# The second product of a squared-ReLU MLP by seven products of halves, with the context's part in a stage of its own

## The chip, the cores and the metric

The kernel runs on one core of one Trainium2 chip as one program. The metric is the device time of one execution in microseconds (us); lower is better. Time before: 4007.97 us, median of three runs (3997.19 to 4012.74).

## The reference, cut to what matters

Two layers of a block with a mixer and an MLP over 1024 tokens of width 1024, and 256 context tokens whose MLP runs in the first layer alone:

```python
def sq_relu_mlp(h, w1, w2):
    a = jax.nn.relu(h @ w1)          # w1: 1024 x 4096
    return (a * a) @ w2              # w2: 4096 x 1024

for l in range(DEPTH):               # DEPTH = 2
    ...
    hx = modulate(rmsnorm(xl, norm2_g[l]), m[:, 3], m[:, 4])
    xl = xl + m[:, 5] * sq_relu_mlp(hx, mlp_w1[l], mlp_w2[l])
    if not last:
        ...
        xc = xc + mc[5] * sq_relu_mlp(hc, mlp_w1[l], mlp_w2[l])
return rmsnorm(xl, final_g)
```

Everything is float32. The change is in the second product, `(a * a) @ w2`, and in what the first one hands to it.

## The kernel before

**Pieces.** The 1024 tokens are two pieces of 512, A and B; the context is a piece C of 256. Activations lie with features on the 128 partitions and tokens along the row, so one matmul has 128 x 128 weights and 512 (C: 256) moving columns.

**Three matmuls for one.** Each float32 operand is cut into a high part (ACT copies it to the matmul's format, L251) and a low part (the difference, on POOL for weights, L291, on DVE for the hidden values, L1771). `mm3` (L254) then issues hi x hi, hi x lo and lo x hi into one bank: called a *three* below.

**Up.** `up` (L1603) makes the hidden values in 16 steps n of two blocks of 128 features, already by seven products of halves of A and B (the weights' sums on DVE, their cuts on ACT and POOL, L1568 to L1582). The products are added on DVE (L1621), squared after the ReLU on DVE (L1625) or ACT, and four results of a step are stored to DRAM in `h` (one of two blocks for one piece each), with two for C.

**Down.** `mlp` (L1785) runs `down` (L1799) over groups of four blocks of w2's rows (at the end groups of two); for each group over the pieces A, C, B (layer 1: A, B) and the eight output blocks b, with one three for each block of the group. After a group's block DVE adds the bank, times a gate, to the residual (L1544, tiles xrA, xrB, xrC). `down_parts` (L1748) makes ready the next group while this one runs: the hidden values `hraw` are loaded, and cut into mhA, mhB or mhC; a row block of w2 (128 x 1024) is loaded in two pieces of 128 x 512 and cut into whi and wlo. In layer 0 `mod_part` (L459, L462) also runs through both stages: it loads `wmod` and adds it up on DVE and POOL for the next layer's gates.

**The end.** In layer 0 A and C are normed for layer 1 (L534, L545) within the last groups, and B after the last matmul, which layer 1's first product of B needs. In layer 1 the final norm, the transposes (L1863), the last scaling (L1865) and the output follow.

**What sets the order.** The code's order is that in which work is recorded; a scheduler fixes each engine's own order. All DMAs go through SP's queue in program order, over eight semaphore lanes; an issue that must wait for a buffer or a lane keeps everything behind it.

## Time and profile before

| | us |
|---|---|
| median of three runs | 4007.97 (3997.19 to 4012.74) |
| the profiled execution | 4004.61 |
| its span in the profile | 4002.8 |
| PE busy | 3587.2 (90%) |
| down of layer 0, with C | 1775.8 to 2224.6 |
| the next layer's first matmul of B | 2259.6 |
| down of layer 1 | 3631.6 to 3981.6 |

The span is the time from the program's first to its last instruction as the profiler saw it; the rest of the execution lies around it. Places in the span are given in us from its start. Stages follow one another on PE, so a stage is read by itself: its stretch of the span, who is busy all through it, and what PE waits for at its two ends.

### The profile page before, as it was taken

To read this page: it belongs to the slowest core of one execution; us is meant where nothing else is said; L and a number is where in the kernel's file an instruction comes from. 1 tells how busy PE (TensorE), PEld (TensorE's weight loads), DVE (VectorE), ACT (ScalarE), POOL (GpSimd) and SP (SyncE) were. 2 spreads that over 40 slices of the span, in tenths; PEclk is the share of its full clock that TensorE was granted. 3 is DMA by queue.
4 is the path that set the end of the run, shared out by engine and by line. 5 is a ranking of instruction groups with operands and counts; after the bars stand their busy time and mean duration, and the time that the engine had idled before them with its cause. 6 is when DMAs were issued, how large, how long until landed. Compare 5 with 4: busy or idle time off the path is not lost.

```text
span 4002.8 us, 61327 instructions
## 1 busy us (share of the span) xinstructions
PE 3587.2 (90%) x23646; PEld 3007.7 (75%) x23646; DVE 2574.5 (64%) x4120; ACT 1394.9 (35%) x2547; POOL 1381.4 (35%) x982
## 2 busy tenths in 40 slices
...
GB/s 220 113 122 138 124 112 176 144 134 113 138 158 203 89 125 142 135 230 150 91 106 35 82 143 88 120 103 180 111 144 149 157 170 95 116 136 188 87 95 42
DMA packets 511174, 520.56 MB, mean 130 GB/s; under 512 B 34454, under 2 KB 384162, under 8 KB 510882
## 3 DMA queue, kind: packets, MB, share of 16 engines
...
## 4 chain that ended last, share of the span: by engine, by line
PE 54%; DVE 11%; DMA 3%; issue 2%; POOL 2%; ACT 2%; SPq 0%; DVEq 0%; ACTq 0%; POOLq 0%
PE bank L254 53%; DVE iD L835 1%; DVE iE L836 1%; DVE iD L829 1%; DMA wmod<-in_w_mod_dram 1%; DMA wraw<-in_mlp_w_dram 0%; DMA yin<-y 0%; POOL macc L462 0%; PE bank L1195 0%; POOL wlo L291 0%; PE bank L258 0%; POOL ras L1153 0%; DVE nt L275 0%; DVE iF L837 0%; DVE rsv L1327 0%
## 5 line engine op out<-in xcount | busy, mean ns | idle before, releaser
L291 POOL TENSOR_TENSOR wlo<-wraw,whi 128x512 fp32r<-128x512 f32 x360 | 503.1, 1420 | 1251.4 <-ACT whi L251 554.6
L251 ACT ACTIVATE whi<-wraw 128x512 fp32r<-128x512 f32 x360 | 214.2, 623 | 369.1 <-PE bank L254 165.8
L254 PE MATMUL bank<-mhB,whi 128*128 128x512 f32 x1024 | 316.2, 390 | 0.0
L254 PE MATMUL bank<-mhA,whi 128*128 128x512 f32 x1024 | 315.4, 389 | 0.0
L1544 DVE SCALAR_TENSOR_TENSOR xrB<-bank,mod,xrB 128x512 f32<-128x512 f32 x176 | 131.6, 749 | 218.9 <-PE bank L254 218.8
L1568 POOL TENSOR_TENSOR uS<-us,uS 128x512 fp32r<-128x512 f32 x128 | 194.3, 1528 | 194.0 <-ACT uS L251 176.2
L254 PEld LDWEIGHTS bank<-mhA,whi 128*128 128x128 f32 x1024 | 192.1, 188 | 39.7
L254 PEld LDWEIGHTS bank<-mhB,whi 128*128 128x128 f32 x1024 | 191.5, 188 | 39.1
L1544 DVE SCALAR_TENSOR_TENSOR xrA<-bank,mod,xrA 128x512 f32<-128x512 f32 x176 | 130.3, 746 | 121.5 <-PE bank L254 121.3
L1621 DVE TENSOR_TENSOR ms<-bank,ms 128x512 f32<-128x512 f32 x216 | 145.1, 684 | 95.5 <-PE bank L254 88.8
L462 POOL TENSOR_TENSOR macc<-macc,wmod 128x512 f32<-128x512 f32 x84 | 135.8, 1616 | 200.9 <-ACT wmod L251 198.1
L459 DVE SCALAR_TENSOR_TENSOR macc<-wmod,cs,macc 128x512 f32<-128x512 f32 x140 | 141.1, 1008 | 98.4 <-DMA wmod<-in_w_mod_dram 54.1
L254 PE MATMUL bank<-xhA,whi 128*128 128x512 f32 (+1 forms) x480 | 203.6, 425 | 0.0
L254 PE MATMUL bank<-xlA,whi 128*128 128x512 f32 (+1 forms) x480 | 199.6, 417 | 0.3 <-POOL xlA L538 0.3
L254 PE MATMUL bank<-xhA,wlo 128*128 128x512 f32 (+1 forms) x480 | 199.0, 416 | 0.6 <-POOL wlo L291 0.6
L254 PE MATMUL bank<-mhB,wlo 128*128 128x512 f32 x512 | 199.3, 389 | 0.0
L254 PE MATMUL bank<-mhA,wlo 128*128 128x512 f32 x512 | 199.2, 389 | 0.0
L254 PE MATMUL bank<-xhB,whi 128*128 128x512 f32 (+1 forms) x416 | 165.5, 398 | 13.7 <-ACT ru L251 13.7
L702 DVE SCALAR_TENSOR_TENSOR gy<-gu,vt,gy 128x1282 f32<-128x1282 f32 (+1 forms) x96 | 154.3, 1607 | 27.1 <-ACT gy L251 26.4
L254 PE MATMUL bank<-xlB,whi 128*128 128x512 f32 (+1 forms) x416 | 164.5, 395 | 0.0
L254 PE MATMUL bank<-xhB,wlo 128*128 128x512 f32 (+1 forms) x416 | 164.3, 395 | 0.0
L1568 POOL TENSOR_TENSOR uA<-wraw,uA 128x512 fp32r<-128x512 f32 x96 | 140.4, 1472 | 60.3 <-ACT uA L251 57.5
...
## 6 DMA issues: line engine op xcount, KB each, us to landing
...
wraw<-in_w_in_dram SPq DMA_DIRECT2D x100, 256.0 KB
...
```

The source lines that it names most:

```text
L251: return self.S.activation(out, in_, func, **kw)
L254: return self.nc.tensor.matmul(out, lhsT, rhs, start=start, stop=stop)
L291: self.P.tensor_tensor(lo[:, o + i:o + i + m], raw, h.bitcast(F32), SUB)
L459: V.scalar_tensor_tensor(acc[:, 0], raw, c[0], acc[:, 0], MUL, ADD)
L462: P.tensor_tensor(acc[:, 1], acc[:, 1], raw, ADD)
L702: V.scalar_tensor_tensor(y[:, a:b], u[:, a + t:b + t], w(t), y[:, a:b], MUL, ADD)
L829: (V.tensor_copy if d else self.act)(lane(D, 3 * d, i, 4), lg[d][q[i], :, q[i]])
L835: V.tensor_tensor(t, F[:, m:, j:m].to_broadcast([128, n, m]), E[:, j:m, :m].to_broadcast([128, n, m]), MUL)
L836: V.tensor_tensor(E[:, m:, :m], E[:, m:, :m], t, SUB)
L1544: self.V.scalar_tensor_tensor(x, ps, self.lv[self.l]["m"][:, mo + b, i:i + 1], x, MUL, ADD)
L1568: self.P.tensor_tensor(t[:, 1], w, t[:, 0].bitcast(F32), SUB)
L1621: V.tensor_tensor(out, ps, s, ADD)
```

## The change

**Seven products for eight.** `halves_down` takes w2 in halves (of the hidden features even and odd blocks, of the output blocks 0 to 3 and 4 to 7) and the tokens in halves A and B, and forms the eight products of halves by seven. It runs 112 steps in each layer: two halves f of the hidden features, seven products p, eight pairs of blocks n. A step holds one sum of weights cut in two (`wu`, 128 x 512) and one part of the hidden values cut in two (`hu`, 128 x 512) and does four threes of 512 columns, one into each of four banks, which gather over the eight n. At n == 7 the banks are added into the running sums `ms` or into the residual (`out`). The weights lie whole as loaded (`we`, `wo`, 128 x 1024 each, eight of both); their sums are made on DVE at p == 1 (in the recorded order), one of them in tiles `ws`, and f = 1's weights are loaded into the same tiles at p == 3 and p == 6.

**Up stores seven parts.** Each step of `up` stores the four results and three differences of them (T1 to T4 with T4 in the next step), made on DVE; three of the four squares are on ACT now.

**The context first.** `context_down` does C's product before, in 32 iterations of eight threes of 256 columns, a column block of w2 at a time (wraw pieces of 128 x 4 x 128: rows of 512 bytes), with one of the two low parts on DVE. C is then normed for layer 1, and stored.

**The end.** The squares of B's blocks 4 to 7 are made before the last product's banks, those of 0 to 3 after it.

```diff
+HALVES = ("B11", "B21", "T2", "T3", "T4", "T1", "B22")
+DOWN = ("A11", "A12", "S2", "S3", "A22", "S1", "S4")
...
-                self.P.tensor_tensor(lo[:, o + i:o + i + m], raw, h.bitcast(F32), SUB)
+                (self.V if even and i else self.P).tensor_tensor(lo[:, o + i:o + i + m], raw, h.bitcast(F32), SUB)
...
-        if j:
+        if len(sq) > 1:
...
+        def keep(t, n, i):
+            self.store(self.dram(f"h{l}{n}", (128, 7, 512))[:, HALVES.index(i)], t)
...
+        def square(t):
             self.act(t, t, AF.Relu)
             self.act(t, t, AF.Square)
+            return t
...
+            if rest:
+                c21, t2 = rest.pop()
+                t = tile()
+                V.tensor_tensor(t, c21, t2, SUB)
+                keep(t, n - 1, "T4")
+                self.free(t, c21, t2)
             if ready:
+                c11 = tile()
+                self.load(c11, self.dram(f"h{l}{n}", (128, 7, 512))[:, 0])
                 if n % 2:
                     self.free(s1s[n // 2])
             else:
                 ps = prod("A12", "B21")
                 ctx(0, "A12", 1)
-                third(total(s1, ps, s1), n, 0, 0)
+                c11 = square(total(s1, ps, s1))
+                keep(c11, n, "B11")
...
             u4 = total(tile(), prod("S1", "T1"), u2)
             done("S1")
             ps = prod("S3", "T3")
-            t = total(tile(), ps, u4)
+            c22 = total(tile(), ps, u4)
             total(u2, ps, u2)
-            second(t, n, 1, 512)
+            keep(square(c22), n, "B22")
             done("S3")
-            second(total(u4, prod("S4", "B22"), u4), n, 0, 512)
+            c12 = total(u4, prod("S4", "B22"), u4)
+            V.scalar_tensor_tensor(c12, c12, 0.0, c12, ALU.max, MUL)
             done("S4")
             next(mod, None)
             ps = prod("A22", "T4")
...
                 ctx(1, "A22", 1)
                 ctx(1, "A21", 0)
                 self.free(x["A21"])
+            t1, t2 = tile(), tile()
+            V.tensor_tensor(t1, c12, c11, SUB)
+            keep(t1, n, "T1")
+            V.tensor_tensor(t2, c22, t1, SUB)
+            keep(t2, n, "T2")
+            V.tensor_tensor(c12, c22, c12, SUB)
+            keep(c12, n, "T3")
+            self.free(t1, c11, c22, c12)
             done("A22")
-            second(total(u2, ps, u2), n, 1, 0)
+            c21 = square(total(u2, ps, u2))
+            keep(c21, n, "B21")
+            rest.append((c21, t2))
...
+    def context_down(self, l, mod):
+        V = self.V
         w2 = self.A["mlp_w2"][l].rearrange("(k p) c -> p k c", p=128)
+        hs, ws = [], {}
+        for n in range(16):
+            while not (self.avail["x"] or self.avail["w"]) or n >= 12 and self.upward:
+                yield
+            t = self.slot("mhC", (2, 2, 256), F32R, "a")
+            raw = self.slot("hraw", (2, 256), F32, "r")
+            self.load(raw, self.dram(f"hc{l}{n}", (128, 2, 256)))
             self.act(t[:, 0], raw)
+            V.tensor_tensor(t[:, 1], raw, t[:, 0].bitcast(F32), SUB)
             self.free(raw)
+            hs.append(t)
+            if n % 4 == 3 and n < 12:
+                while len(self.avail["u"]) < 2:
+                    yield
+                ws[n // 4] = self.wsplit(w2[:, n // 4 * 8:n // 4 * 8 + 8, 0:128], kind="u")
+                yield
+        self.back_x(f"xm{l}", "C")
+        for i in range(32):
+            b, c = divmod(i, 4)
+            if i + 3 < 32:
+                d, e = divmod(i + 3, 4)
+                ws[i + 3] = self.wsplit(w2[:, e * 8:e * 8 + 8, d * 128:d * 128 + 128], kind="u", even=True)
+            if c == 0:
+                ps = self.ps("d")[:, :256]
+            hi, lo = ws.pop(i)
+            for k in range(8):
+                t = hs[c * 4 + k // 2]
+                self.mm3(ps, hi[:, k], lo[:, k], t[:, 0, k % 2], t[:, 1, k % 2], c == 0 and k == 0, c == 3 and k == 7)
+            self.free(hi, lo)
+            if b == 7:
+                self.free(*hs[c * 4:c * 4 + 4])
+            if c == 3:
+                self.residual(b, 40)(ps, "C")
+            if i % 2:
+                next(mod, None)
             yield
+    def halves_down(self, l, last):
+        V = self.V
+        w2 = self.A["mlp_w2"][l].rearrange("(k p) c -> p k c", p=128)
+        take = lambda nm, kind, dt=F32: self.slot(nm, (2, 512), dt, kind)
+        steps = [(f, p, n) for f in range(2) for p in range(7) for n in range(8)]
+        raws, us, hs = {}, [], []
+        even, odd, sums = [], [], []
+        def fetch(t, fb):
+            self.load(t, w2[:, fb].rearrange("p (h c) -> p h c", h=2))
+        def fetch_h(i):
+            if i < len(steps):
+                f, p, n = steps[i]
+                raws[i] = self.slot("hraw", (512,), F32, "r")
+                self.load(raws[i], self.dram(f"h{l}{8 * f + n}", (128, 7, 512))[:, p])
+        def ready(i):
+            if i >= len(steps):
+                return
+            f, p, n = steps[i]
+            fetch_h(i + 5)
+            w = {"A11": (even, 0), "A12": (odd, 0), "S2": (even, 0), "S3": (even, 1), "A22": (odd, 1), "S4": (odd, 0)}
+            src = sums[n // 2][:, n % 2] if DOWN[p] == "S1" else w[DOWN[p]][0][n][:, w[DOWN[p]][1]]
+            u, h, raw = us[i % 3], hs[i % 3], raws.pop(i)
+            self.act(h[:, 0], raw)
+            V.tensor_tensor(h[:, 1], raw, h[:, 0].bitcast(F32), SUB)
+            self.free(raw)
+            self.act(u[:, 0], src)
+            self.P.tensor_tensor(u[:, 1], src, u[:, 0].bitcast(F32), SUB)
+            if p == 1:
+                e, o, s1 = even[n], odd[n], sums[n // 2][:, n % 2]
+                V.tensor_tensor(s1, e[:, 1], o[:, 1], ADD)
+                V.tensor_tensor(e[:, 1], e[:, 0], e[:, 1], SUB)
+                V.tensor_tensor(e[:, 0], s1, e[:, 0], SUB)
+                V.tensor_tensor(o[:, 0], o[:, 0], e[:, 0], SUB)
+            for q, ts, o in ((3, even, 0), (6, odd, 1)):
+                if p == q:
+                    if f == 0:
+                        fetch(ts[n], 2 * (n + 8) + o)
+                    else:
+                        self.free(ts[n])
+            if p == 5 and f == 1 and n % 2:
+                self.free(sums[n // 2])
+        def wait(kind, n=1):
+            while len(self.avail[kind]) < n:
+                yield
+        for i in range(8):
+            yield from wait("x")
+            even.append(take("we", "x"))
+            fetch(even[i], 2 * i)
+            if i == 3:
+                for j in range(5):
+                    fetch_h(j)
+        yield
+        for i in range(8):
+            yield from wait("u")
+            odd.append(take("wo", "u"))
+            fetch(odd[i], 2 * i + 1)
+        while self.upward:
             yield
+        yield "turn"
+        for i in range(3):
+            us.append(take("wu", "x", F32R))
+            hs.append(take("hu", "xuu"[i], F32R))
+        ready(0)
+        ready(1)
+        u2, u3 = ([take("ms", "x") for _ in range(2)] for _ in range(2))
+        sums += [take("ws", "w!") for _ in range(4)]
+        half = lambda t, b: t[b // 2][:, b % 2]
+        def out(b, pc, ps, s):
+            t = self.slot("mt", (512,), kind="r")
+            V.tensor_tensor(t, ps, s, ADD)
+            x = self.block(self.xr[pc], b)
+            V.scalar_tensor_tensor(x, t, self.lv[self.l]["m"][:, 40 + b, 0:1], x, MUL, ADD)
+            self.free(t)
+        for i, (f, p, n) in enumerate(steps):
+            ready(i + 2)
+            if n == 0:
+                ps = [self.ps("d") for _ in range(4)]
+            u, h = us[i % 3], hs[i % 3]
+            for b in range(4):
+                c = slice(b * 128, b * 128 + 128)
+                self.mm3(ps[b], u[:, 0, c], u[:, 1, c], h[:, 0], h[:, 1], n == 0, n == 7)
+                if n == 7:
+                    a, z = half(u2, b), half(u3, b)
+                    nm = DOWN[p]
+                    if nm == "A11":
+                        self.act(a, ps[b])
+                    elif nm == "A12":
+                        out(b, "A", ps[b], a)
+                    elif nm == "S2":
+                        V.tensor_tensor(a, ps[b], a, ADD)
+                    elif nm == "S3":
+                        V.tensor_tensor(z, ps[b], a, ADD)
+                    elif nm == "A22":
+                        out(b + 4, "A", ps[b], z)
+                    elif nm == "S1":
+                        V.tensor_tensor(a, ps[b], a, ADD)
+                        out(b + 4, "B", ps[b], z)
+                    else:
+                        out(b, "B", ps[b], a)
+            if f == 1 and n == 7 and p == 5:
+                self.free(*u3)
+            yield f, p, n
+        self.free(*u2, *us, *hs)
     def mlp(self, l, last):
         mod = iter(()) if last else self.mod_part(l + 1, 0, 48)
+        down = self.halves_down(l, last)
+        self.upward = True
+        if last:
+            self.up(l, last, mod, down)
+        else:
+            ctx = self.context_down(l, mod)
+            self.up(l, last, mod, ctx)
+            turn = ""
+            for i, _ in enumerate(ctx):
+                if i > 8 and not turn:
+                    turn = next(down)
+            for _ in mod:
+                pass
+            self.gains(l + 1, 1)
+            self.rstat("C")
+            self.norm(l + 1, 1, "C")
+            self.save_x(f"x{l + 1}", "C")
+            del self.xr["C"]
+        while last and next(down) != "turn":
+            pass
+        for p in "AB":
             self.back_x(f"xm{l}", p)
+        sq = []
+        for f, p, n in down:
+            if f == 0:
+                continue
+            if (p, n) == (5, 1):
                 self.rstat("A")
+            if (p, n) == (5, 7) and not last:
+                self.first = [self.wsplit(self.win(l + 1, c), kind="w!") for c in (768, 256)]
+            if (p, n) == (6, 0):
+                if not last:
+                    self.norm(l + 1, 1, "A")
+                for j in (2, 3):
+                    self.squares("B", j, sq)
+        for j in range(2):
+            self.squares("B", j, sq)
+        self.rsum("B", sq)
         if not last:
             self.norm(l + 1, 1, "B")
```

**SP, layer 0, about the end of up.** Names are the tile written, then what is read: hraw are hidden values, wraw a weight piece, wmod the gates' weights, we and wo the whole row blocks of w2. Before:

```order
L261 DMA hraw<-h_10711 128x2x256
L261 DMA hraw<-h_10770 128x2x256
L261 DMA hraw<-h_10711 128x512 x2
L261 DMA hraw<-h_10770 128x512 x2
L261 DMA wmod<-in_w_mod_dram 128x512 x5
L261 DMA hraw<-h_11600 128x512
L261 DMA wraw<-in_mlp_w_dram 128x512 x2
L261 DMA hraw<-h_11600 128x512
L261 DMA wraw<-in_mlp_w_dram 128x512 x2
L261 DMA hraw<-h_11830 128x512
```

After, the loads that follow the last ones of the context's stage:

```order
L264 DMA wraw<-in_mlp_w_dram 128x4x128 x8
L264 DMA wmod<-in_w_mod_dram 128x512 x3
L264 DMA wraw<-in_mlp_w_dram 128x4x128 x4
L264 DMA wmod<-in_w_mod_dram 128x512 x3
L264 DMA wraw<-in_mlp_w_dram 128x4x128 x2
L264 DMA wmod<-in_w_mod_dram 128x512 x2
L264 DMA wo<-in_mlp_w_dram 128x1024 x2
L264 DMA we<-in_mlp_w_dram 128x1024 x2
L264 DMA wo<-in_mlp_w_dram 128x1024 x6
L267 DMA x_15725<-xrC_14422 128x4x256
L267 DMA x_15725<-xrC_14423 128x4x256
L264 DMA xrA_15728<-xm_10026 128x2x512
```

The weights of the halves' stage (wo and the last two we, 512 KB each) stand behind all loads of the context's stage, and the reload of the residual (xrA and on) behind them.

**DVE, layer 0, from the context's last bank to the second step of the halves.** In the rows of after L1849 is a sum of the last weights loaded, L277 to L279 the last rounds of the rsqrt, L537 and L548 the norm of C, L1842 the low part hu of a step. Before, a steady stretch of down:

```order
L1544 SCALAR_TENSOR_TENSOR xrB_14200<-bank_70,mod_116,xrB_14200 128x512
L1544 SCALAR_TENSOR_TENSOR xrB_14201<-bank_71,mod_116,xrB_14201 128x512
L1771 TENSOR_TENSOR mhA<-hraw,mhA 128x512
L1544 SCALAR_TENSOR_TENSOR xrB_14201<-bank_72,mod_116,xrB_14201 128x512
L471 TENSOR_TENSOR mod_117<-bank_74,vt_114 128x4
L1771 TENSOR_TENSOR mhA<-hraw,mhA 128x512 x2
L1544 SCALAR_TENSOR_TENSOR xrA_14186<-bank_67,mod_116,xrA_14186 128x512
```

After:

```order
L1849 TENSOR_TENSOR we<-we 128x512
L279 SCALAR_TENSOR_TENSOR rst_2_360<-nt_0_366,rst_2_360 128x2
L277 TENSOR_TENSOR nt_0_366<-rst_2_360 128x2
L278 TENSOR_TENSOR nt_0_366<-nt_0_366,nh_0_368 128x2
L279 SCALAR_TENSOR_TENSOR rst_2_360<-nt_0_366,rst_2_360 128x2
L537 SCALAR_TENSOR_TENSOR nt<-xrC_14422,g_1_131,bank_73 128x256 x3
L548 SCALAR_TENSOR_TENSOR xlC_15685<-nt,mod_117,xhC_15683 128x256
L537 SCALAR_TENSOR_TENSOR nt<-xrC_14422,g_1_131,bank_73 128x256
L548 SCALAR_TENSOR_TENSOR xlC_15685<-nt,mod_117,xhC_15683 128x256
L537 SCALAR_TENSOR_TENSOR nt<-xrC_14423,g_1_131,bank_73 128x256 x4
L548 SCALAR_TENSOR_TENSOR xlC_15686<-nt,mod_117,xhC_15684 128x256
L1842 TENSOR_TENSOR hu<-hraw,hu 128x512
```

The second step's hu now stands behind that sum and nearly the whole norm of C; before, an mhA has only residuals and the gates' sums about it.

**DVE, after, in layer 0 from the first half f = 0 to f = 1** (before's down has no such sums; its steady rows stand above):

```order
L1848 TENSOR_TENSOR ws<-we,wo 128x512 x2
L1842 TENSOR_TENSOR hu<-hraw,hu 128x512
L1849 TENSOR_TENSOR we<-we 128x512 x2
L1848 TENSOR_TENSOR ws<-we,wo 128x512 x2
L1842 TENSOR_TENSOR hu<-hraw,hu 128x512
L1849 TENSOR_TENSOR we<-we 128x512 x2
L1848 TENSOR_TENSOR ws<-we,wo 128x512
L1842 TENSOR_TENSOR hu<-hraw,hu 128x512
L1849 TENSOR_TENSOR we<-we 128x512
L1848 TENSOR_TENSOR ws<-we,wo 128x512 x2
L1849 TENSOR_TENSOR we<-we 128x512
L1842 TENSOR_TENSOR hu<-hraw,hu 128x512
```

Four steps' hu stand here with thirteen sums of f = 1's weights; with the rows up to the next hu it is five steps and sixteen sums.

## Rows read from the trace of the kernel before

**Rows 1.** Stretches of up's start, up, down (layer 0), down (layer 1), and their columns.

```profile
core 0: us, PE busy (x) PEld busy (x) DVE busy (x) ACT busy (x) POOL busy (x), PEclk, DMA share, GB/s
...
1350.00:1400.00 50.00, 39.29 (x183) 31.22 (x182) 46.39 (x58) 29.32 (x53) 27.60 (x17) 0.83 0.32 96
1500.00:1600.00 100.00, 100.00 (x543) 86.80 (x542) 62.24 (x77) 40.06 (x74) 61.67 (x42) 1.00 0.44 140
...
1876.00:1976.00 100.00, 100.00 (x536) 86.81 (x535) 54.54 (x73) 19.78 (x35) 24.59 (x16) 1.00 0.37 116
3736.00:3836.00 100.00, 100.00 (x443) 82.84 (x442) 43.15 (x57) 20.55 (x36) 22.92 (x16) 1.00 0.32 100
```

**Rows 2.** Line L254 over the span: count, durations, first and last start.

```profile
L254 PE MATMUL bank<-mhA,whi x1024: 387/389/486, 1775.8 to 3968.5; 128*128 128x512 f32 x171
```

**Rows 3.** Groups of layer 0's MLP (1335 to 2260): C's matmuls.

```profile
L254 PE MATMUL bank<-mhC,whi 128*128 128x256 f32 x512 | 92.8, 284 | 0.1
```

**Rows 4.** Timeline of PE: threes of 512 (layer 1's first) and of 256 columns.

```profile
2203.68 0.40 PE L254 MATMUL bank<-mhC,whi 128*128 128x256 f32 x2
...
2205.84 0.40 PE L254 MATMUL bank<-mhC,whi 128*128 128x256 f32 x2
...
3631.64 0.62 PE L254 MATMUL bank<-mhA,whi 128*128 128x512 f32 x2
...
3633.68 0.62 PE L254 MATMUL bank<-mhA,whi 128*128 128x512 f32 x2
```

**Rows 5.** The page's groups: busy, mean ns of one, idle before.

```profile
L291 POOL TENSOR_TENSOR wlo<-wraw,whi 128x512 fp32r<-128x512 f32 x360 | 503.1, 1420 | 1251.4 <-ACT whi L251 554.6
L251 ACT ACTIVATE whi<-wraw 128x512 fp32r<-128x512 f32 x360 | 214.2, 623 | 369.1 <-PE bank L254 165.8
...
L1544 DVE SCALAR_TENSOR_TENSOR xrA<-bank,mod,xrA 128x512 f32<-128x512 f32 x176 | 130.3, 746 | 121.5 <-PE bank L254 121.3
```

**Rows 6.** Timelines of DVE and of POOL in up, 1644 to 1647 us.

```profile
1644.32 1.76 DVE L1574 TENSOR_TENSOR us<-wraw 128x512 f32<-128x512 f32 x1 [1.19 <-POOL uS L1568]
...
1646.61 0.68 DVE L1575 TENSOR_TENSOR us<-us,wraw 128x512 f32<-128x512 f32 x1
...
1644.24 1.30 POOL L1568 TENSOR_TENSOR uA<-wraw,uA 128x512 fp32r<-128x512 f32 x1
```

**Rows 7.** Stretches with DMA at full load; columns as in rows 1.

```profile
1174.00:1182.00 8.00, 6.79 (x37) 5.36 (x35) 6.50 (x21) 4.75 (x8) 3.53 (x3) 1.00 1.11 298
...
1780.00:1800.00 20.00, 20.00 (x100) 16.97 (x99) 9.24 (x12) 8.67 (x14) 9.11 (x6) 1.00 1.01 347
1800.00:1820.00 20.00, 19.88 (x124) 17.86 (x124) 16.57 (x25) 5.32 (x9) 3.75 (x3) 1.00 0.80 267
```

**Rows 8.** Timeline of SP ahead of the first of these stretches: the loads issued.

```profile
1173.38 9.31 SPq L261 DMA_DIRECT2D wraw<-in_w_out_dram  x8
```

**Rows 9.** Timelines at layer 0's end: last down matmul, norms, B's first.

```profile
2224.25 0.39 PE L254 MATMUL bank<-mhB,wlo 128*128 128x512 f32 x1
...
2232.78 1.06 ACT L251 ACTIVATE sq<-xrB 128x1024 f32<-128x1024 f32 x1 [0.62 <-DVE xrB L1544]
...
2236.12 1.23 DVE L496 TENSOR_TENSOR sq<-sq 128x1024 f32<-128x1024 f32 x1
...
2237.40 2.31 PE L254 MATMUL bank<-cst,sq 128*128 128x1 f32 x16 [1.14 <-DVE sq L496]
...
2240.28 1.26 DVE L534 SCALAR_TENSOR_TENSOR nt<-xrC,g,bank 128x256 f32<-128x256 f32 x3 [0.16 <-PE bank L258]
...
2245.13 0.70 DVE L270 TENSOR_SCALAR rst<-rsm 128x4 int32<-128x4 int32 x1
...
2249.65 2.06 DVE L534 SCALAR_TENSOR_TENSOR nt<-xrB,g,bank 128x512 f32<-128x512 f32 x3 [1.43 <-PE bank L258]
...
2259.62 0.79 PE L254 MATMUL bank<-xhB,whi 128*128 128x512 f32 x1 [9.77 <-ACT ru L251]
```

**Rows 10.** Timeline of PE at layer 1's end: the first transposes.

```profile
3981.65 4.23 PE L1863 MATMUL bank<-cst,xrA 128*128 128x128 f32 x32
```

115 lines of the change are left out of this document (16 added, 99 removed).

## The prediction

> **What bounds the kernel now.** I read stretches by stage first, since the changed stage has a bound of its own. In the middle of down PE is busy 100.00 of 100 us in both layers at a granted clock of 1.00, with DVE at 43 to 55, POOL at 23 to 25 and DMA at about a third of its share [rows 1]. So this stage costs what its matmuls cost, and nothing else. Up, just ahead, is also PE at 100.00, but with DVE and POOL at 62 each [rows 1]. The reader should then see the price of a three: from 3631.64 to 3633.68 lie three of them, 0.68 us each [rows 4]; six of C's lie between 2203.68 and 2205.84, 0.36 us each [rows 4]. Last, the ends of the stages: layer 0's down runs from 1775.8 [rows 2] to 2224.25 and the next matmul of B comes at 2259.62 after 9.77 us without work [rows 9]; layer 1's runs from 3631.64 [rows 4] to 3981.65, where the transposes begin [rows 10], with 21.2 us to the span's end at 4002.8.
>
> **What is removed.** The 1024 matmuls mhA,whi [rows 2] are 512 threes' hi parts in two layers (two a three); B has as many, so a layer has 512 threes of A and B: 512 x 0.68 = 348.2 us. Seven products for eight make 448: 304.6 us. That is 43.5 us a layer, 87 us in all. C's 256 threes (512 matmuls with whi [rows 3]) stay, 256 x 0.361 = 92.4 us. The rest is what the new arrangement gives back.
>
> **A step of the halves: 12 matmuls, 2.72 us.** Per step ACT cuts two tiles, 2 x 0.62 = 1.25; POOL makes one low part, 1.42; DVE one, 0.68 to 0.75 [rows 5, 6]. Each is under 2.72, and three buffers give a chain two steps, 5.44 us, against ACT 0.62 + POOL 1.42 = 2.0. Loads are 0.26 MB a step, 97 GB/s, and weights besides: under the 116 and 100 GB/s of down now, to twice that [rows 1], against 267 to 347 at full load [rows 7]. So steady steps are PE's. At a product's end DVE adds four banks, with up to three operations each (0.68 to 0.75 us [rows 5, 6]): 6 to 9 us, while PE goes on into other banks; I take 4 us a layer for the thirteen such ends, 0 to 10.
>
> **From f = 0 to f = 1.** The order of after has 16 sums of weights and 5 hu on DVE in five steps: 21 x 0.68 = 14.3 us against 13.6 of PE, were DVE alone. But DVE's operation of two operands took 1.76 us beside a POOL operation of 1.30 that began with it, and 0.68 us alone [rows 6]. The longer one is the shorter plus 1.08, nearly the POOL operation. Five POOL low parts at 1.3 then make 14.3 + 6.5 = 20.8, 7 us more than PE's five steps. Some slack is left by the buffers: I take 5 us a layer, 0 to 10. The Trainium skill ("SBUF — State Buffer", "SBUF: two separate sides") says that DVE with two SBUF inputs and POOL exclude each other for a whole instruction; rows 6 agree. Without such a rule this term would be about 1 us, and the sum 8 us lower.
>
> **Context stage (layer 0).** PE needs 92.4 us and some 4 for the small matmuls of the gates. But the 29 iterations after up's end issue, by the order, 58 weight pieces (15.2 MB), 32 wmod (8.4), 6 we (3.1) and 5 hraw (1.3): 28 MB. Eight w_out pieces of the same shape (128 x 4 x 128) ran at 298 GB/s [rows 7, 8]; mixed loads at 347, and 267 in the next 20 us [rows 7]. 28 MB take 81, 94 or 105 us; with 8.7 us for the first three iterations, prefetched, 90, 103 or 114. I take 100, between PE's own and the 298 row, its closest kin; 94 to 114.
>
> **Turn to the halves (layer 0).** Step 1 needs its hu, which stands on DVE behind the last weights' sum and C's norm. The ten loads wo and we are 5.2 MB behind all the context's: 15 us at 347, 18 at 298, from about 6 us before the context's last matmul, so 9 to 12 after it. Behind these come on DVE what is left of the rsqrt (in before 2245.13 to 2248.2 plus 1.43 us for its spread) and eight nt and four xl of C, 2240.28 to 2245.13 = 4.85 us [rows 9]; 6 to 8 us. Together 15 to 20, less step 0's 2.72: 12 to 17. C's own chain without DMA (square 1.06, sum 1.23, ones 2.31, rsqrt 3.1, spread 1.4, norm 4.85 [rows 9]: 14) gives 11. I take 16, bounds 10 to 25, since a granted clock under 1 after idling (0.83 where PE was busy 39.29 of 50 [rows 1]) may add some.
>
> **A's norm (layer 0)** comes into DVE's order ahead of a hu at the last product's start: eight nt and four xl at about 0.75 = 9 us, less two steps of slack: 6 us, 0 to 9.
>
> **End of layer 0.** Before: 2224.25 to 2259.62 = 35.4 us, since B's square sums and rsqrt stood behind C's norm on DVE. After: the last banks 4.5 us behind the last matmul, square 1.06, sum 1.23, ones 2.3, rsqrt 3.1 and its ends 0.8, spread 1.4, and from B's first nt to PE as now 10.0 (2249.65 to 2259.62) [rows 9]: 24; one of these overlaps PE's transposes, so 23, 20 to 28. A gain of 12, covered by A's and C's matmuls only as far as these reach.
>
> **Layer 1.** At the turn the hidden values of step 5 are loaded on SP behind the last stores of up and 12 reloads of the residual (4 MB, 13 us at 307 GB/s, the mean of the two later rows [rows 7]), some 18 to 20 us after up's end; PE wants them at 13.6: 7 us, 2 to 10. At the end DVE has four banks of out, not one residual, in front of the last squares: 4 us, 0 to 7.
>
> **Up.** Three more stores of 0.26 MB and about 2 us more of DVE and ACT per n, 19 us long, where DVE and ACT have room [rows 1]. At its start, PE busy 39.29 of 50 [rows 1], DVE is less free: 4 us in both layers, 0 to 10.
>
> **The sum.** Layer 0, from down's first matmul to B's first of layer 1: 483.8 us before; after 100 + 16 + (304.6 + 4 + 5 + 6) + 23 = 459: 25 less. Layer 1 from 3631.64 to the end: 371.2; after 7 + 304.6 + 4 + 5 + 25 = 346: 26 less. With up's 4: 47 less. The profiled execution took 4004.61 us, 3.4 under the median of 4007.97 whose runs lie 15 us apart; 4004.6 - 47 = 3958, and I say 3960 for a median.
>
> **Rivals.** (1) *Nearly the full gain*: DMA keeps to 347 GB/s, the turn is C's chain alone, and buffers hide the rest: 96 + 11 + 308 + 20 = 435 (49 less), and layer 1 at 3 + 306 + 22 = 331 (40 less): 4004.6 - 89 = 3916. For it: PE's 100.00 through every stage with DVE and POOL at 62 [rows 1]. Against: one queue with three kinds of loads. (2) *No change*: DMA runs at the 267 GB/s row, the context takes 114, the turn 25, and both f turns, A's norm and the ends go to their upper bounds: layer 0 at 114 + 25 + 330 + 28 = 497 (13 more), layer 1 at 10 + 325 + 28 = 363 (8 less), up 10: 4004.6 + 15 = 4020; half way there, 3990 to 4015. (3) *Slower*: the hand-over from ACT to POOL to PE sets the step. In p = 0 and 1 a step has a hu and a sum on DVE and a low part on POOL, one after the other: 0.68 x 2 + 1.3 = 2.66, 0.06 under PE's 2.72. If waits of 0.2 us at each change of hands are added to all steps, and POOL's mean of 1.42 and DVE's 0.75 [rows 5] hold, a step is 3.5. It decides from 2.72 + 87/224 = 3.11 us a step, where the whole gain of 224 steps is gone. If only the 64 steps of p = 0, 1 ran at 3.5, 50 us go: 4008, no change; if all at 3.3, 130 us go: 4004.6 - 47 + 130 = 4088. Against: up has POOL and DVE at 62 each and PE still at 100 [rows 1]. That the change does less than it says is excluded by the order: 2688 matmuls of 512 columns for 3072.
>
> **How the numbers follow.** Forecast, 3930 to 3988: 0.60. Rival 1: 0.15. Rival 2: 0.14. Rival 3: 0.11, of which 0.02 end within the bound of no change. About 0.5%, 20 us, is what can be told from none. Faster 0.75, same 0.16, slower 0.09. The range reaches from halfway into rival 1 to halfway into rival 2: 3925 to 4005.
>
> **What would show it.** Right: hu,wu matmuls at 2.72 us a step and PE at 100 in steady products; in the context stage DMA at a share near 1.0 and PE waiting for whi or wlo; 10 to 25 us of idle PE behind step 0 of layer 0, put down to hu; some 5 us at the last eight steps of f = 0; B's first matmul about 23 us after the last of the halves. Wrong: steps over 3 us in a whole product; idle PE at every product's end, put down to the banks' readers; or an up that takes more than 10 us longer.

## The result: slower by 1.1 %, and the profile after

The changed kernel took 4051.11 us (median; 4046.97 to 4051.76), the kernel before 4006.68 on the same chip: a ratio of 1.011 (95% interval 1.009 to 1.0132). The profiled spans are 4049.0 and 4002.8 us. The forecast was 3960, faster.

The top of the page after: the span, the busy time of each engine with its share and count, and the load queue.

```profile
span 4049.0 us, 61967 instructions
...
PE 3543.5 (88%) x23262; PEld 2960.9 (73%) x23262; DVE 2767.0 (68%) x4221; ACT 1619.7 (40%) x2947; POOL 1552.1 (38%) x1113
...
q1 hardware_dynamic: 562210, 585.86, 45.9%
```

The matmuls saved are there, but 12% of the span has no PE work. Where it lies shows only by stage. The table cuts both spans at starts of matmuls in PE's timeline: up's first T2 product, the first matmul of down, the end of layer 0's halves, B's first matmul of layer 1, up's first in layer 1, and so on. Its last column is a second trace of the kernel before (`b1_before`).

| stretch, us | before | forecast | after | difference | before again |
|---|---|---|---|---|---|
| to up, layer 0 | 1363.1 | same | 1359.1 | -4.0 | 1354.2 |
| up, layer 0 | 412.6 | +2 | 451.6 | +39.0 | 412.5 |
| down, layer 0, to B's next matmul | 483.9 | 459 | 487.0 | +3.1 | 483.7 |
| mixers of layer 1, to up | 1066.4 | same | 1073.9 | +7.5 | 1073.2 |
| up, layer 1 | 305.6 | +2 | 309.6 | +4.0 | 305.6 |
| down, layer 1 | 349.8 | 321 | 342.7 | -7.1 | 349.8 |
| from the last product to the end | 21.4 | 25 | 25.2 | +3.8 | 21.4 |

The differences make 46.3; the spans differ by 46.2. The mixers' 7.5 need not be the change's: the kernel before has 1073.2 there in its second trace. So up of layer 0 lost 39 us, and the two downs together gave back almost none of the 51 that were forecast.

**Down.** PE's rows by tile (durations min/median/max, first and last start, the commonest form):

```profile
L257 PE MATMUL bank<-mhC,whi x512: 277/283/584, 1810.7 to 1915.6; 128*128 128x256 f32 x171
...
L257 PE MATMUL bank<-hu,wu x2688: 387/389/797, 1916.7 to 4023.8; 128*128 128x512 f32 x192
```

The context runs from 1810.7 to 1916.7, 106.0 us. Then come the halves, 359.5, and the end, 21.5: 487.0. Stretches of after, with the columns of [rows 1]: all of layer 0's up, 50 us of its start, the context's middle, and steady halves:

```profile
1359.00:1810.00 451.00, 402.72 (x2014) 342.41 (x2013) 283.94 (x349) 190.34 (x352) 226.83 (x154) 0.91 0.49 160
1400.00:1450.00 50.00, 40.05 (x188) 33.64 (x188) 31.25 (x37) 20.25 (x37) 27.86 (x20) 0.83 0.48 158
1850.00:1900.00 50.00, 44.73 (x350) 44.23 (x349) 29.35 (x36) 22.72 (x36) 22.28 (x17) 0.93 0.99 290
1960.00:2060.00 100.00, 100.00 (x443) 82.81 (x442) 66.06 (x68) 42.68 (x74) 47.72 (x37) 1.00 0.40 129
```

The last row is the plan at work: PE at 100.00, with DVE at 66 and POOL at 48 under it. The starts of the matmuls there give 2.72 us a step. The context is bound by DMA, at a share of 0.99. The first row is the trouble: PE is busy 402.72 of 451, while no other engine reaches two thirds. The same stretch of the kernel before:

```profile
1363.00:1775.00 412.00, 389.79 (x2013) 333.70 (x2012) 254.61 (x311) 157.33 (x284) 233.58 (x156) 0.95 0.45 143
```

Idle PE is 48.3 us against 22.2, 26 more. The other 13 are busy time, for the same 2013 matmuls: the granted clock fell from 0.95 to 0.91. PE's waits in up, after and then before (total, times, longest). The helpers' lines lie three further on in after: a matmul is L257, a load L264, a store L267 there, and L254, L261 and L264 before. T1 to T4 with h or l behind them, as in T2h, are up's own operands and not the parts that it stores.

```profile
PE bank L257 <- DVE macc L462: 30.6, 6, 10.2
PE bank L257 <- ACT T2h L254: 6.6, 2, 3.5
PE bank L257 <- POOL macc L465: 5.7, 4, 2.7
```

```profile
PE bank L254 <- DVE macc L459: 7.2, 2, 4.9
...
PE bank L254 <- POOL macc L462: 4.1, 2, 2.2
```

`macc` is the running sum of the gates for layer 1 (two `next(mod)` in each step's order, from `mod_part`). PE adds it up over the partitions with 128x1 matmuls that stand at the start of a product; when `macc` is late, the product behind it waits. 36.3 against 11.3 us: the 25 between them are nearly all of the 26 us of added idle time. One of these waits, first on PE, then on DVE, then on SP's queue (start, duration, operation, idle before):

```profile
1452.48 0.39 PE L257 MATMUL bank<-T4h,uA 128*128 128x512 f32 x1
1463.10 0.59 PE L257 MATMUL bank<-cst,macc 128*128 128x1 f32 x2 [10.23 <-DVE macc L462]
1463.55 0.77 PE L257 MATMUL bank<-T4l,uA 128*128 128x512 f32 x1
```

```profile
1460.30 2.75 DVE L462 SCALAR_TENSOR_TENSOR macc<-wmod,cs,macc 128x512 f32<-128x512 f32 x2 [1.42 <-DMA wmod<-in_w_mod_dram]
```

```profile
1440.70 0.33 SPq L264 DMA_DIRECT2D wmod<-in_w_mod_dram  x1
1445.26 0.33 SPq L267 DMA_DIRECT2D h<-ms  x1
1446.85 0.38 SPq L264 DMA_DIRECT2D wraw<-in_mlp_w_dram  x1
1449.10 2.03 SPq L267 DMA_DIRECT2D h<-ms  x2
1451.22 0.39 SPq L264 DMA_DIRECT2D wraw<-in_mlp_w_dram  x1
1451.72 0.49 SPq L267 DMA_DIRECT2D h<-ms  x1
...
1453.95 1.38 SPq L264 DMA_DIRECT2D wraw<-in_mlp_w_dram  x2
1455.91 1.23 SPq L264 DMA_DIRECT2D wmod<-in_w_mod_dram  x2
```

The reader should follow it from below: SP issues in order. Between one `wmod` load and the next lie 15 us, with six stores `h<-ms` and `hc<-mt` between; each can go only when DVE or ACT has made its tile, and weights' pieces (`wraw`) and `wmod` stand behind. So DVE gets `wmod` late, `macc` is late, and PE stands for 10.23 us in the middle of a product whose first matmul has run. That reading is of one wait. SP's waits in up, summed, show less: after and then before,

```profile
SPq L264 <- POOL macc L465: 64.1, 19, 10.0
SPq L267 <- ACT ms L254: 47.5, 19, 5.2
SPq L267 <- DVE ms L1751: 45.0, 12, 6.1
```

```profile
SPq L264 <- DVE ms L1625: 87.4, 36, 6.0
SPq L264 <- ACT mt L251: 62.7, 20, 8.7
SPq L261 <- POOL macc L462: 46.3, 17, 6.8
```

The queue waited for stores' tiles before as well, and no less. What grew are waits of its loads for buffers that POOL was the last to use: with `macc` from 46.3 to 64.1 us, with `uA` from 11.8 to 31.9. So lateness of the gates may feed itself. Whether the stores start it takes experiments (e2 and e9).

**The halves, step by step.** Eight steps without a loss take 21.76 us. What each product took beyond that, from the starts of its matmuls:

| place | forecast | layer 0 | layer 1 |
|---|---|---|---|
| first product | 16 (turn) / 7 | 19.5 | 18.3 |
| f = 0's last and f = 1's first product | 5 | 9.3 | 10.2 |
| f = 1, p = 5: A's square sums | not listed | 10.0 | 8.65 |
| f = 1, p = 6: A's norm (layer 0 alone) | 6 | 16.3 | 1.1 |
| the other nine products | 4 for all ends | 0.0 | 0.0 |
| sum | 31 / 16 | 55.1 | 38.3 |

PE at p = 5 and 6 of layer 0:

```profile
2218.48 3.57 PE L257 MATMUL bank<-cst,sq 128*128 128x1 f32 x16 [3.57 <-DVE sq L499]
...
2262.09 13.13 PE L257 MATMUL bank<-hu,wu 128*128 128x512 f32 x50 [11.26 <-DVE hu L1842]
```

The first is the same pattern as `macc`: small matmuls of A's square sums stand in PE's order ahead of ready steps. In the second, twelve operations of A's norm and a sum of B's squares stand on DVE ahead of a `hu`, and PE runs dry for 11.26 us.

### The profile page after: what moved, and what is told of

Same layout as the page of the kernel before. It is cut to its first block, busy times and chain, and to the rows that moved or that the text cites. A ratio compares the mean times of both kernels' runs of the same rounds, so it can differ in the third digit from the quotient of the medians.

```text
span 4049.0 us, 61967 instructions
## 1 busy us (share of the span) xinstructions
PE 3543.5 (88%) x23262; PEld 2960.9 (73%) x23262; DVE 2767.0 (68%) x4221; ACT 1619.7 (40%) x2947; POOL 1552.1 (38%) x1113
## 5 line engine op out<-in xcount | busy, mean ns | idle before, releaser
L257 PE MATMUL bank<-hu,wu 128*128 128x512 f32 x2688 | 634.7, 398 | 40.9 <-DVE hu L1842 21.0
L294 POOL TENSOR_TENSOR wlo<-wraw,whi 128x512 fp32r<-128x512 f32 x267 | 359.8, 1365 | 756.9 <-ACT whi L254 378.8
L257 PEld LDWEIGHTS bank<-hu,wu 128*128 128x128 f32 x2688 | 513.5, 192 | 160.1 <-DVE hu L1842 28.3
L1842 DVE TENSOR_TENSOR hu<-hraw,hu 128x512 fp32r<-128x512 f32 x224 | 267.8, 1199 | 145.2 <-ACT hu L254 140.2
L254 ACT ACTIVATE whi<-wraw 128x512 fp32r<-128x512 f32 (+1 forms) x296 | 179.8, 625 | 195.8 <-DMA wraw<-in_mlp_w_dram 50.1
L254 ACT ACTIVATE ms<-ms 128x512 f32<-128x512 f32 x176 | 110.4, 627 | 269.7 <-DVE ms L1624 254.4
L257 PE MATMUL bank<-xhA,whi 128*128 128x512 f32 (+1 forms) x480 | 204.7, 428 | 0.0
L257 PE MATMUL bank<-xlA,whi 128*128 128x512 f32 (+1 forms) x480 | 201.3, 421 | 0.0
L1845 POOL TENSOR_TENSOR wu<-we,wu 128x512 fp32r<-128x512 f32 x96 | 137.6, 1434 | 163.1 <-ACT wu L254 156.8
L257 PE MATMUL bank<-xhA,wlo 128*128 128x512 f32 (+1 forms) x480 | 199.8, 417 | 0.3 <-POOL wlo L294 0.3
L1845 POOL TENSOR_TENSOR wu<-wo,wu 128x512 fp32r<-128x512 f32 x96 | 130.1, 1355 | 142.6 <-ACT wu L254 138.0
L257 PE MATMUL bank<-xhB,whi 128*128 128x512 f32 (+1 forms) x416 | 164.3, 395 | 5.0 <-ACT ru L254 5.0
L257 PE MATMUL bank<-xlB,whi 128*128 128x512 f32 (+1 forms) x416 | 163.7, 394 | 0.0
L257 PE MATMUL bank<-xhB,wlo 128*128 128x512 f32 (+1 forms) x416 | 163.1, 392 | 0.0
L838 DVE TENSOR_TENSOR iD<-iF,iE 128x31 f32<-128x31 f32 (+15 forms) x310 | 147.6, 477 | 6.6
L839 DVE TENSOR_TENSOR iE<-iE,iD 128x31 f32<-128x31 f32 (+15 forms) x310 | 145.8, 471 | 6.5
```

Of the source, the lines that this page charges most:

```text
L254: return self.S.activation(out, in_, func, **kw)
L257: return self.nc.tensor.matmul(out, lhsT, rhs, start=start, stop=stop)
L294: (self.V if even and i else self.P).tensor_tensor(lo[:, o + i:o + i + m], raw, h.bitcast(F32), SUB)
L838: V.tensor_tensor(t, F[:, m:, j:m].to_broadcast([128, n, m]), E[:, j:m, :m].to_broadcast([128, n, m]), MUL)
L839: V.tensor_tensor(E[:, m:, :m], E[:, m:, :m], t, SUB)
L1842: V.tensor_tensor(h[:, 1], raw, h[:, 0].bitcast(F32), SUB)
```

## Experiments

Each row is a kernel that differs from the changed one by the edit shown or named below. Spans and stretches are from one profiled execution each, cut as above; `halves` are without the context.

| kernel | span | up 0 | context | halves 0 | up 1 | down 1 |
|---|---|---|---|---|---|---|
| after | 4049.0 | 451.6 | 106.0 | 359.5 | 309.6 | 342.7 |
| e2_four_stores | 4008.4 | 423.3 | 107.2 | 359.9 | 307.1 | 333.3 |
| e3_no_sums_up | 3995.0 | 413.2 | 106.5 | 359.7 | 305.6 | 330.7 |
| e1_mod_late | 4023.0 | 418.2 | 96.3 | 374.4 | 308.1 | 343.3 |
| e8_act_stores | 4047.8 | 445.1 | 108.7 | 359.8 | 311.0 | 341.0 |
| e9_t_late | 4036.1 | 431.3 | 106.1 | 358.3 | 311.7 | 348.6 |
| e11_mod_pace | 4027.6 | 438.5 | 105.6 | 361.3 | 309.2 | 342.9 |
| e4_rsum_norm | 4023.5 | 445.7 | 105.9 | 343.0 | 307.7 | 337.1 |
| e5_residual_late | 4032.9 | 448.3 | 106.6 | 358.4 | 307.5 | 337.2 |
| e6_cnorm_late | 4048.3 | 449.3 | 105.8 | 352.2 | 307.0 | 337.3 |
| e7_no_sums_f1 | 4025.0 | 451.0 | 105.8 | 354.6 | 308.0 | 335.0 |
| e10_sums_spread | 4044.6 | 445.3 | 107.9 | 355.0 | 307.6 | 341.7 |
| v3 | 3986.2 | 431.7 | 106.5 | 331.1 | 308.4 | 326.4 |
| v5 | 3980.6 | 428.5 | 109.1 | 331.5 | 309.8 | 326.1 |

Spans are not to be compared closer than some 20 us: the stretches that no edit touches (up to layer 0's up, 1349 to 1371; the mixers, 1066 to 1084) move by as much. e6 is a case: its up began at 1371.3, so its span shows none of what its halves won. The verdicts below go by the stretch that the edit touches. That has its own scatter: e4, e5, e6, e7 and e10 leave up as it is in after, and their up of layer 0 took 445.3 to 451.0 us against 451.6, so a difference of some 6 us there shows nothing.

**The kernel before again.**

> The kernel before once more, for a second trace: from B's first matmul of layer 1 to up's first T2 product it took 1066.4 us, the changed kernel and its variants 1073 to 1080. If the difference lies in the change (order and placement of code and DMAs), 1064 to 1069; if it varies from run to run, anything up to 1080.

Span 4000.4, with the stretches of the last column of the first table. MLP stretches of this kernel repeat within 0.2 us; the mixers do not. A difference of that size in the mixers need not be an effect of the change.

### Up: what makes `macc` late

**T2, T3 and T4 made but not stored** (left out; the halves read other parts in their place).

```diff
 def keep(t, n, i):
+    if i in ("T2", "T3", "T4"):
+        return
```

> The changed kernel, where up makes the sums T2, T3 and T4 but does not store them (four stores a step, as before); the halves read stored parts in their place, so that part of the computation is left out. Theory 1 (the queue): layer 0's up falls from 451.6 us to 425 or less. Theory 2 (DVE and ACT): it stays at 440 or more, since every sum and square is still made.

Up took 423.3, 28.3 less.

**The four differences T1 to T4 not made either** (left out; four parts are stored, and the reload of B11 that T1 needs in the first four steps is gone too).

> The same, where up does not make T1 to T4 either (no sums on DVE, no reload of B11 in the first four steps; c12 is stored as the fourth part); the halves read stored parts in their place, so that part of the computation is left out. Theory 1: within 8 us of the kernel with four stores. Theory 2: 415 us, at least 20 us under it.

Up took 413.2: 10.1 less again, which lies between the two theories, and 0.6 from the kernel before. So of 39 us, three stores with the buffers that they hold are 28, and the sums on DVE with that reload 10. Up of e2 and of e3:

```profile
1355.00:1779.00 424.00, 391.55 (x2024) 335.64 (x2024) 285.79 (x346) 190.17 (x349) 226.58 (x154) 0.94 0.44 141
```

```profile
1358.00:1771.00 413.00, 388.95 (x2017) 333.32 (x2016) 226.23 (x286) 193.40 (x349) 220.65 (x154) 0.95 0.45 142
```

In e2 DVE and ACT are as busy as in after, 286 and 190 us; PE's busy time falls by 11 and its idle time by 16. Busy engines alone are not the cause.

PE's waits for `macc` by their place say more. Before 1500 they make 20.8 us in after, 21.3 in e2, 13.6 in e3 and 11.2 in the kernel before; behind 1500 they make 15.5 in after, 0.4 in e2 and none in the other two. The last one of after, and in e2 the one in the place of that of 10.23 us:

```profile
1800.80 1.86 PE L257 MATMUL bank<-cst,macc 128*128 128x1 f32 x8 [6.70 <-DVE macc L462]
```

```profile
1456.96 0.58 PE L257 MATMUL bank<-cst,macc 128*128 128x1 f32 x2 [6.95 <-DVE macc L462]
```

So the three stores account for the later waits. The early ones, the one followed above among them, stay without these stores; what makes them longer than before goes with the sums and the reload.

**The gates taken out of up's way**: one call in a step instead of two, and the other 32 of their 48 parts in the halves' odd steps.

```diff
-            next(mod, None)
...
-        mod = iter(()) if last else self.mod_part(l + 1, 0, 48)
+        mod = iter(()) if last else self.mod_part(l + 1, 0, 16)
+        late = iter(()) if last else self.mod_part(l + 1, 16, 48)
...
+            if i >= 8 and i % 2:
+                next(late, None)
```

> The changed kernel with the next layer's gates moved: up advances them once a step instead of twice (four groups of 128 x 512 columns of w_mod), the context's stage not at all, and the other eight groups run in the steps of layer 0's halves. Theory 1 (the seven stores of a step stand in SP's queue ahead of the loads of w_mod, so that the sums macc come late, and PE, which runs in order, waits at the matmul that adds them up) and theory 2 (DVE and ACT are too full with the new sums and squares, so macc is late) both expect layer 0's up, from the first matmul of T2 to the first of the context's down, at 415 us or less (451.6 in the changed kernel, 412.7 before), and PE's waits for macc there at under 8 us (36.3 now). The context's stage loses 8.4 MB: 97 us instead of 106. The span comes to about 4005 us (4049.0). Rival: the lost time of up has nothing to do with the gates (stores, sums or the clock alone), and up stays above 440.

Up took 418.2 (415 or less was expected), 33.4 less. That shows the gates on the path, but not how much of the 39 goes through them: half of their work has left this up, and with it waits that the kernel before has too (11.3 us). Waits of PE in up of this kernel:

```profile
PE bank L257 <- ACT mt L254: 14.6, 4, 4.7
...
PE bank L257 <- POOL macc L465: 2.1, 1, 2.1
```

Those for `macc` fell from 36.3 to 2.3, but 14.6 us for `mt` came up, 1.5 in after. The context came down to 96.3, since its `wmod` loads are gone, against some 92.4 us that its matmuls cost [rows 3, 4]. The halves paid 15 us for the gates there. A wait that is moved is not a wait that is gone.

**Stores of what ACT makes issued by ACT's queue**, those of the T's left on SP.

```diff
-            self.store(self.dram(f"h{l}{n}", (128, 7, 512))[:, HALVES.index(i)], t)
+            q = self.nc.sync if i[0] == "T" else self.nc.scalar
+            q.dma_start(self.dram(f"h{l}{n}", (128, 7, 512))[:, HALVES.index(i)], t)
```

> The changed kernel with the stores of ACT's own results in up (B11, B22, B21 and the two of the context) issued from ACT's DMA queue; T1 to T4, made on DVE, stay on SP's. All data are stored. Theory 1 (stores that wait in SP's queue hold up the loads of w_mod behind them): layer 0's up falls from 451.6 us to about 425, as with four stores on SP's queue, and layer 1's first product by 5 us or more. Span about 4015. Theory 1b (it is the DMA engines' share that seven stores take, not their place in a queue): up stays at 440 or more.

A miss: up 445.1, 6.5 less, which is what up moves by without an edit to it. The stores of the T's stayed on SP, which still waited 76.3 us for T1's tiles from DVE there. As far as one run tells, the stores of ACT's results were not the ones in the way.

**Stores of T1 to T3 later**: queued with T4, behind the next step's S2 product, when DVE has long made them.

```diff
-            keep(t1, n, "T1")
...
-            keep(t2, n, "T2")
...
-            keep(c12, n, "T3")
...
+                for t, i in ((t1, "T1"), (t2, "T2"), (t3, "T3"), (c21, "T4")):
+                    keep(t, n - 1, i)
```

> The changed kernel with the stores of T1, T2 and T3 put behind the next step's S2 product, beside T4's (their tiles are held that long); all seven parts are stored, by SP's queue. Theory 1 in its narrower form (the stores that wait for DVE's sums stand in SP's queue ahead of the next weights and of w_mod): layer 0's up falls from 451.6 us to 430 or less, and layer 1's first product by 4 us or more. Rival (the DMA time of seven stores, or DVE's time for the sums): up stays at 445 or more.

Up took 431.3 (430 or less was expected), 20.3 less, with all seven parts made and stored: with as many bytes, and tiles held longer (T4 alone is made in place, with a tile fewer), the place of the stores in the queue is what was dear. PE's waits for `macc` are 17.5 us before 1500 and 4.5 behind it, so here too it is mostly the later ones that went. They still lead PE's waits in up:

```profile
PE bank L257 <- DVE macc L462: 18.9, 3, 9.0
```

Layer 1's first product, which had been expected to gain 4 us or more, became worse, 23.0 for 18.3, probably since up's last stores are now nearer to the loads of the halves.

**The gates paced**: one call in each of the first four steps, two then, three in steps 8 to 11.

> The changed kernel with the gates' pace in layer 0's up changed and nothing else: one call a step in the first four steps (which are short), two in the next, three in steps 8 to 11; 32 calls in all, as before. If what is left of up's loss lies in those early steps, where a group's loads and sums have half the time before PE comes to its matmul: PE's waits for macc before 1500 us fall from 20.8 us to under 6, and up falls from 451.6 by 12 us or more. Rival (the later waits grow by as much, since the loads are late wherever they stand): up stays at 445 or more.

Up took 438.5, 13 less. The waits for `macc` before 1500 fell from 20.8 to 3.8 us, but the later ones stayed, 16.3 us for 15.5 (3.5, 6.4 and 4.6 the longest). Pacing helps and does not cure.

### Down: what stops the halves

**A's square sums and norm moved.** The ones matmuls of A's squares go from p = 5, n = 1, where the squares are made, to n = 5; A's norm is done a block in a step of p = 6 rather than all in its first, and the squares of B's blocks 4 to 7 go to n = 2 and 4 there.

```diff
-                self.rstat("A")
+                sa = []
+                for j in range(4):
+                    self.squares("A", j, sa)
+            if (p, n) == (5, 5):
+                self.rsum("A", sa)
...
-                    self.norm(l + 1, 1, "A")
+            if p == 6:
+                next(na, None)
```

> The changed kernel with A's square sums added up on PE four steps later than the squares are issued (steps 1 and 5 of the sixth product of f = 1 instead of both at step 1), and A's norm in layer 0 a block a step through the last product instead of all ahead of its first step. Theory (small matmuls and DVE blocks of the norms stand in PE's and DVE's order ahead of the next steps): the sixth product of f = 1 falls from 31.8 and 30.4 us (layers 0 and 1) to 24 or less, the last product of layer 0 from 38.0 to 30 or less, the span from 4049 to about 4025. Rival (the DVE work itself is too much for these 16 steps, wherever it stands): both together fall by less than 8 us.

At p = 5 the loss fell from 10.0 to 1.9 (layer 1: 8.65 to 1.9), at p = 6 from 16.3 to 5.9; layer 0's halves took 343.0 for 359.5. In the row that answers to the one at 2218.48 PE goes on without idle time:

```profile
2219.72 1.84 PE L257 MATMUL bank<-cst,sq 128*128 128x1 f32 x16
```

The end grew from 21.5 to 25.7, probably since the last of A's norm and of B's squares are nearer to it.

**The residual reloaded later**: A's eight blocks after step 3, B's in the third product.

```diff
-        for p in "AB":
-            self.back_x(f"xm{l}", p)
...
+            if (f, p, n) == (0, 0, 3):
+                self.back_x(f"xm{l}", "A")
+            if (f, p, n) == (0, 2, 0):
+                self.back_x(f"xm{l}", "B")
```

> The changed kernel with the reloads of the residual put later: A's behind the fourth step of the halves, B's behind the second product, instead of ahead of the first step. Theory (12 reloads stand in SP's queue ahead of the hidden values of the sixth step in layer 1): layer 1's first product falls from 40.1 us to about 31; steps 0 and 1, which wait for DVE, keep their 9.7 us over 2.72 each. Layer 0's first product stays at 41 us. Span 4040 us. Rival (the hidden values wait for up's last stores, not for the reloads): less than 3 us.

Layer 1's first product lost 11.5 for 18.3; layer 0's 19.0 for 19.5. The start of layer 1's halves, in after and in e5:

```profile
3685.83 0.96 PE L257 MATMUL bank<-hu,wu 128*128 128x512 f32 x3 [2.04 <-DVE ms L1624]
...
3692.44 12.11 PE L257 MATMUL bank<-hu,wu 128*128 128x512 f32 x46 [4.06 <-DVE hu L1842]
3710.01 5.36 PE L257 MATMUL bank<-hu,wu 128*128 128x512 f32 x11 [5.46 <-ACT hu L254]
```

```profile
3675.47 8.29 PE L257 MATMUL bank<-hu,wu 128*128 128x512 f32 x28 [2.54 <-DVE ms L1624]
...
3685.62 2.79 PE L257 MATMUL bank<-hu,wu 128*128 128x512 f32 x11 [0.62 <-POOL wu L1845]
3691.39 20.96 PE L257 MATMUL bank<-hu,wu 128*128 128x512 f32 x84 [2.98 <-DVE hu L1842]
```

The late wait for ACT's `hu`, which waits for its load, is gone: that part was the reloads in SP's queue, as forecast, worth 7 us. The early ones stay. SP in after, where up's last matmul started at 3680.91:

```profile
3691.21 1.44 SPq L267 DMA_DIRECT2D h<-ms  x3
...
3696.03 6.94 SPq L264 DMA_DIRECT2D xrB<-xm  x8
3703.36 8.30 SPq L264 DMA_DIRECT2D hraw<-h  x12
```

Up's last stores go out 10 us and more behind its matmuls, and stand ahead of the reloads and these loads. With three stores fewer, all sums still made, the product lost 8.9 (e2); without the sums as well, 5.0 (e3).

**C's norm later too**: e5, and C's mean square in the second product's step 1, its norm in step 4.

> As the kernel with later reloads, and C's square sums and norm for layer 1 moved into the second product of layer 0's halves. Theory A (C's norm stands on DVE ahead of the second step): layer 0's first product falls from 41.3 us to 30 or less (21.8 would be no loss), with up to 5 us lost in the second product. Theory B (the last weight blocks wo, loaded behind the context's own, end last): it falls by 5 us at most.

Layer 0's first product lost 5.0 for 19.5 (19.0 in e5): 14 us of the turn are C's square sums and norm, as forecast. But the second and third product lost 2.96 and 3.25, so the net was 7 us, and 6 against e5.

**No sums of weights for f = 1** (left out).

```diff
-            if p == 1:
+            if p == 1 and f == 0:
```

> The changed kernel without the sums of weights of f = 1 (the weights are loaded as they are), so that part of the computation is left out. Theory (16 sums and 5 low parts on DVE beside POOL's low parts take longer than five steps of PE): the last product of f = 0 and the first of f = 1 lose together 2.5 us or less over 43.5 (9.3 in layer 0 and 10.2 in layer 1 now). Rival (the loss is that of the four banks read at a product's end, or of late reloads of weights): 7 us or more stay.

The loss around f = 1's start fell from 9.3 and 10.2 to 1.9 in both layers: all but that is the sums. DVE there in after:

```profile
2077.41 2.39 DVE L1848 TENSOR_TENSOR ws<-we,wo 128x512 f32<-128x512 f32 x2
2079.72 0.68 DVE L1842 TENSOR_TENSOR hu<-hraw,hu 128x512 fp32r<-128x512 f32 x1
2080.32 2.38 DVE L1849 TENSOR_TENSOR we<-we 128x512 f32<-128x512 f32 x2
2082.61 2.38 DVE L1848 TENSOR_TENSOR ws<-we,wo 128x512 f32<-128x512 f32 x2
```

and POOL beside it:

```profile
2080.34 1.80 POOL L1845 TENSOR_TENSOR wu<-wo,wu 128x512 fp32r<-128x512 f32 x1 [1.70 <-ACT wu L254]
```

Two sums take 2.38 where a low part runs on POOL, and 1.36 would be twice the 0.68 of the row between. The row of [rows 6] was no accident. The prediction's rule from the Trainium skill ("SBUF — State Buffer", "SBUF: two separate sides"), that DVE with two SBUF inputs and POOL exclude each other for a whole instruction, agrees with these rows.

**The sums spread** over p = 1, 2 and 3: two, one and one in a step.

> The changed kernel with the same sums of weights recorded over three products (two a step at p = 1, one at p = 2, one at p = 3) instead of four a step at p = 1. Theory (DVE's pile of sums about the first products): last product of f = 0 and first of f = 1 lose 4 us or less together (9.3 and 10.2 now), and layer 1's first product falls from 40.1 us by 3 us or more, since fewer sums stand ahead of its second step. Rival (POOL and DVE are too full in any of these steps): the loss moves into p = 2 and 3, and the halves' time changes by less than 4 us a layer.

9.3 became 6.9 and 10.2 became 6.9, where 4 or less had been expected. Layer 1's first product, 19.2, did not gain.

### Together

`v3` joins e9, e4, e6 and e10; `v5` adds e11.

> All of it together: late stores of T1 to T3, late reloads, C's norm in the second product, sums spread, A's square sums apart and its norm a block a step. If the losses add up as read one by one: up of layer 0 at 430 us, halves of layer 0 at 328 and of layer 1 at 320 us, span about 3975 us, 0.7% under the kernel before. Rival (each stall taken away uncovers the next one on DVE): 4003 us or more, no better than before.

> The combined kernel with that pace too. If the early steps are the cause: up of layer 0 falls from 431.7 us to 418 or less, the span from 3986 to about 3972, some 0.9% under the kernel before. Rival: up stays at 428 or more and the span at 3983 to 3990.

v3: 3988.07 against 4007.9, a ratio of 0.994 (0.9913 to 0.9966). v5: 3982.01 against 4008.41, 0.9928 (0.9906 to 0.9951): by 0.7% faster than the kernel before, with an interval that leaves out 1, and by more than the changed one. The span of v3 was expected at 3975 and came at 3986.2. In v5 layer 0's halves come to 331.5 and layer 1's to 326.1, near the forecast for them (336 with the turn, and 321). Up remains at 428.5 where 418 were expected; waits of PE in up of v5:

```profile
PE bank L257 <- DVE macc L462: 12.5, 4, 5.0
...
PE bank L257 <- POOL macc L465: 3.9, 2, 1.9
```

These 16.4 are 5 above the kernel before; other waits and the clock make the rest of the 16 us by which up is still longer.

## Why the prediction was wrong

The forecast said -47, the traces say +46. The 93 us between them: 39 in the two ups, 28 in layer 0's down, 22 in layer 1's, 3.5 in stretches whose code the change does not touch.

- **Removed matmuls and the step of 2.72 us**: right. Nine products of fourteen in layer 0 and as many in layer 1 run without any loss, so rival 3 (a dearer step) is refuted, and a slower kernel came by another way. The 4 us a layer for the products' ends were 0.
- **Up, 4 us in both layers**: the step that failed. It was argued from shares: "where DVE and ACT have room". It did not list what stands behind the new stores on SP's queue (the gates' weights), nor what stands behind the gates' small matmuls on PE. It was 39.0 in layer 0: 28 from the stores, and 10 from the sums with the reload of B11 (e2, e3), which the term does not name; 25 of it as waits for the gates (36.3 against 11.3), which e1 took away with half of their work; 20 by the stores' place (e9). In layer 1, whose up has neither gates nor context beside it, the same stores and sums cost 4.0.
- **The clock**: the forecast gave a bound for it at the turn alone. In up, 26 us more of idle PE came with a granted clock of 0.91 for 0.95, and 39 us were lost.
- **A's square sums, not listed**: 10.0 and 8.65. The prediction counted the small matmuls where PE had run out of work anyway (the turn, the end), not where they stand ahead of ready steps.
- **A's norm, 6 us**: 16.3. Two steps of slack were allowed for (9 less two steps of 2.72 would be 3.6 and not 6); the twelve operations took about the 9, but the slack was not there: PE ran dry for 11.26 us. Spreading it gave 10.4 back (e4).
- **Turn of layer 0, 16**: 19.5, within its bounds of 10 to 25, and 14 of it are C's square sums and norm (e6). That its cost would come back in part in later products was not foreseen.
- **Start of layer 1, 7, bounds 2 to 10**: 18.3. The reloads in SP's queue, the only part that the term priced, are 7 of it (e5: 11.5 are left; its own 18 to 20 less 13.6 makes 4 to 6). Up's last stores stand ahead of them in the term, but without a price: three stores fewer leave 8.9 (e2). What up leaves on DVE, which the term did not have, is 4 of it (e3: 5.0 are left). The parts overlap, and no run has stores and reloads out of the way at once.
- **Start of f = 1, 5, bounds 0 to 10**: 9.3 and 10.2. Mechanism right (e7), size too small by half, and in layer 1 just over the bound; "some slack is left by the buffers" did not hold.
- **Context, 100, bounds 94 to 114**: 106.0, bound by DMA at 0.99 and 290 GB/s, near the 298 that the price was made from. **Ends, 23 and 25**: 21.5 and 25.2.

Rival 2 had the downs about right, 497 and 363 for 487.0 and 367.9, but by luck: its context of 114 and turn of 25 were 106.0 and 19.5, and A's square sums, which it did not have, came in their place. (Its 330 for layer 0's halves should be 334 by its own bounds.) No rival had up. The sign in the prediction's last part, an up that takes more than 10 us longer, is what came.

Open: which of several in-order chains holds the last 16 us of up when everything is made and stored. Each edit there moved part of the wait to a later step or to another operand (e1: `mt`; v5: 12.8 us for `macc` behind 1500, 5.0 in v3). That the stores act through SP's queue rests on e2 and e9, one run each; v3, with e9's up, repeats it at 431.7. The one wait followed through the queue does not show it, since its like stays in e2; SP's summed waits do not either; and e8, which took other stores off that queue, shows no gain. Stores of the T's on a queue of their own were not run.
